# A first gather of four experts straight from unsplit tokens, and a branch hint, in a two-layer attention and MoE kernel

## The chip, the cores and the metric

One core of a Trainium2 chip. The metric is the device time of one execution in microseconds; the engines are TensorE (PE, with its weight loads as PEld), VectorE (DVE), ScalarE (ACT), GpSimd (POOL) and SyncE (SP), which issues the DMAs.

## The reference

A decoder trunk of two layers on 256 tokens of 1024 fp32 values. Each layer has a mixer (three kinds of attention, gated and summed) and a mixture of 16 experts:

```python
for l in range(DEPTH):
    y = mixer(x, w_in[l], a_w_uk[l], a_w_uv[l], c_sinks[l], w_branch[l], w_o[l], cos, sin)
    x = layer_norm(DN_ALPHA * x + y, ln1_g[l], ln1_b[l])
    y = moe(x, router_w, router_b, moe_w_gate[l], moe_w_up[l], moe_w_down[l])
    x = layer_norm(DN_ALPHA * x + y, ln2_g[l], ln2_b[l])

def moe(x, ...):
    aff = sigmoid(xt @ router_w); sel_score = aff + router_b
    # 4 groups of 4 experts: the group whose best two scores sum highest, and in it the best two experts
    ...
    for e in range(N_EXPERTS):
        he = jax.nn.silu(xt @ w_gate[e]) * (xt @ w_up[e])
        y = y + combine[:, e:e + 1] * (he @ w_down[e])
```

w_gate and w_up are 1024 x 512 for each expert, w_down 512 x 1024; all is fp32.

## The kernel before

Everything that is large lives in one pool of 25 slots of 1 MB (8 KB on each partition). Weights come in loads of 1 MB (half of one expert's matrix) in the order of their use, all issued on SP's queue. A load is issued by pump(), as long as fewer than 25 - target["o"] slots hold weights; target["o"] is the number of slots kept for other tiles. put() gives slots back after a product and pumps again. A load waits on SP until the last reader of its slot is done, and at most eight loads are outstanding.

**Mixer's end (L838 to L874).** The last stage adds the output product to the residual in four pieces (half h, token tile t), takes statistics of each (stat), and forms the router's products (logits). ln_scales gives mean and 1/std of a token tile (DVE, then POOL).

**MoE's start (L938 to L1035).** WARM[0] transposes keep PE busy. normed() normalizes a token tile in place (xv is the view [token, tile, q, k], column = 8 q + k), high() casts it to x1h (fp32r, ordered by k), low() forms x1l = x - x1h on POOL and DVE. In between stand the router's steps on DVE: sigmoid (aff), sel, pr, gsum, gmax, gr, best, mx, msk. One product (L1012, `pc`) counts the tokens ahead of each in its expert, and onehot(0) (L1028) turns that into Sx, the one-hots of the first eight experts, 32 places each, for both token tiles.

**gather(r) (L1039).** For eight experts: for each of 8 k and 2 token tiles, a product with x1h[:, t, k] and one with x1l[:, t, k] as the stationary operand (128 x 128, packed) and Sx (256 columns) moving; ACT and DVE evict to xe with LayerNorm's gain and shift. gather(0) runs its first four k ahead of the first gate product and the others behind that product's first half (L1190); gather(1) runs at pair 3 (L1346).

**Main loop (L1311).** For pairs p = 0 to 7 of experts: gate product up_("g", p), up product up_("u", p), each in two halves q of 16 products; tanh and multiplications on ACT and DVE (he); from p = 1 on, down(p - 1), which multiplies by w_down in two halves with turn(p) (transposes of he) between. accumulator(0) at p = 1 has POOL rebuild the tokens as x1h + x1l. slot_maps(0) and turn(0) stand behind the gate product of p = 1. The last down product has rest() between its halves, which issues eight products by an identity (ah, al). At p = 7, over() (L1192) reads a flag and skips, by a branch (tc.If, L1196), a block for experts with more than 32 tokens; in layer 0 this stands behind the last up product, in layer 1 at the start of p = 7. The block is skipped with these inputs.

Each compute instruction goes through a helper, so its line in the profile is L163; each DMA's is L221. A row is told apart by its tile.

Of the kernel before, what the change touches and what calls it, by code (L numbers as in the profile page):

```python
# [18 lines left out]
D = 1024  # L19
# [17 lines left out]
WARM = [38, 6, 12]  # L37
# [167 lines left out]
def kernel(ctx: ExitStack, tc: tile.TileContext, x, w_in, a_w_uk, a_w_uv, c_sinks, w_branch,  # L205
# [28 lines left out]
    def drop(n=1, kind="o"):  # L234
        held[kind] -= n
# [163 lines left out]
    def ln_shift(mean, rstd):  # L399

        sh = small(1, "sh")
        V.scalar_tensor_tensor(sh, mean, -1.0, rstd, op0=OP.mult, op1=OP.mult)
        return sh
# [26 lines left out]
    def mixer(l, todo):  # L430
# [363 lines left out]
        for i, (c, q) in enumerate(stages):  # L794
# [43 lines left out]
            if i == len(stages) - 1:  # L838
                def piece(h, t):

                    cs, ts = slice(256 * h, 256 * h + 256), slice(128 * t, 128 * t + 128)
                    o = pa[c][2 * h + t][:, :256]
                    for kk in range(2):
                        k = 2 * q + kk
                        PE.matmul(o, lh[:, k, ts], hl[:, 0, kk, cs], start=False, stop=False)
                        PE.matmul(o, ll[:, k, ts], hl[:, 0, kk, cs], start=False, stop=False)
                        PE.matmul(o, lh[:, k, ts], hl[:, 1, kk, cs], start=False, stop=(kk == 1))
                    z = xt[0][:, t, 512 + 256 * h:768 + 256 * h]
                    V.scalar_tensor_tensor(z, z, ALPHA, o, op0=OP.mult, op1=OP.add)

                def stat(h, t):
                    V.bn_stats(st[t][:, 12 + 6 * h:18 + 6 * h], xt[0][:, t, 512 + 256 * h:768 + 256 * h])

                halves = (range(2), range(2, 4))
                piece(0, 0)
                piece(0, 1)
                stat(0, 0)
                piece(1, 0)
                stat(0, 1)
                logits(0, 1, 0, halves[0])  # L860
                piece(1, 1)
                logits(1, 1, 0, halves[0])
                logits(0, 1, 0, halves[1])
                stat(1, 0)
                sc = ln_scales(st[:1])
                logits(0, 1, 1, halves[0])
                logits(1, 1, 0, halves[1])
                logits(1, 1, 1, halves[0])
                logits(0, 1, 1, halves[1])
                logits(1, 1, 1, halves[1])  # L870
                stat(1, 1)
                sc += ln_scales(st[1:])
                drop(3)
                return sc, lg, rsum  # L874
# [63 lines left out]
    def moe(l, sc, lg, rsum):  # L938
        target["o"] = 5
        pump()  # L940


        xh = slot([128, T, KD, 128], F32R, "x1h")
        xl = slot([128, T, KD, 128], F32R, "x1l")
        warm(WARM[0])
        xv, hv, lv = xt[0].rearrange("p t (q k) -> p t q k", k=KD), xh.rearrange("p t k q -> p t q k"), \
            xl.rearrange("p t k q -> p t q k")
        halves = [slice(0, 512), slice(512, 1024)]

        def normed(t, k):  # L950
            z = xv[:, t, :, k:k + 4]
            if t == 0:
                V.tensor_scalar(z, z, sc[0][0], sc[0][1], op0=OP.subtract, op1=OP.mult)
            else:
                A.activation(z, z, AF.Identity, bias=sh, scale=sc[1][1])

        def high(t, k):
            A.copy(hv[:, t, :, k:k + 4], xv[:, t, :, k:k + 4])

        def low(E, t, k):  # L960
            E.tensor_tensor(lv[:, t, :, k:k + 4], xv[:, t, :, k:k + 4], hv[:, t, :, k:k + 4].bitcast(F32), op=OP.subtract)

        aff, sel = small(32, "aff"), small(64, "sel")
        z = [aff[:, NE * t:NE * t + NE] for t in range(T)]
        normed(0, 0)
        high(0, 0)
        low(G, 0, 0)
        for t in range(T):
            V.scalar_tensor_tensor(z[t], rsum[:, 0:NE], sc[t][0], lg[t][:, 0:NE], op0=OP.mult, op1=OP.subtract)
        for t in range(T):  # L970
            V.scalar_tensor_tensor(z[t], z[t], sc[t][1], rsum[:, NE:2 * NE], op0=OP.mult, op1=OP.subtract)
        A.activation(aff, aff, AF.Exp)
        sh = ln_shift(*sc[1])
        normed(1, 0)
        normed(0, 4)
        high(0, 4)
        high(1, 0)
        normed(1, 4)
        high(1, 4)
        low(G, 0, 4)  # L980
# [33 lines left out]
        low(V, 1, 0)  # L1014
# [6 lines left out]
        def onehot(r):  # L1021

            Sx[r] = work((128, 8, T, CAP), F32R, name="Sx")
            for t in range(T):
                z = (pos if r else pc)[:, NE * t + 8 * r:NE * t + 8 * r + 8, None].to_broadcast([128, 8, CAP])
                V.tensor_tensor(Sx[r][:, :, t], cc("iota")[:, None, :].to_broadcast([128, 8, CAP]), z, op=OP.is_equal)
# [10 lines left out]
        xe = {}  # L1037

        def gather(r, ks=range(KD)):  # L1039

            if r not in xe:
                z = [slot([128, 4, 8, T, CAP], F32, "xe") for i in range(2)]
                xe[r] = [z[k // 4][:, k % 4] for k in range(KD)]
            for k in ks:
                o = (ptp if k % 2 == 0 else psc)()
                ov_ = o.rearrange("p (e t s) -> p e t s", t=T, e=8)
# [131 lines left out]
        def up_(nm, p, o):  # L1178
            def product(k, a, w):
                x_ = xe[p // 4][k][:, 2 * (p % 4) + a].rearrange("p t s -> p (t s)")  # L1180
                PE.matmul(o[64 * a:64 * a + 64], x_, w, start=(k == 0), stop=(k == KD - 1))

            for q in range(2):
# [5 lines left out]
                if (nm, p, q) == ("g", 0, 0):  # L1189
                    gather(0, range(4, KD))  # L1190

        def over():  # L1192
# [3 lines left out]
            with tc.If(flag > 0):  # L1196
# [8 lines left out]
                with tc.For_i(0, NE, 1) as e:  # L1205
# [5 lines left out]
                    for k in range(KD):  # L1211
                        for j, z in enumerate((xh, xl)):
# [98 lines left out]
        for p in range(NE // 2):  # L1311
            if p == 1:
                target["o"] = 6
            if p == 2:
                target["o"] = 7
# [9 lines left out]
            up_("g", p, pg)  # L1325
            if p == 1:
                slot_maps(0)
                turn(0)
# [14 lines left out]
            if p % 4 == 3:  # L1343
                drop(2)
            if p == 3:
                gather(1)  # L1346
# [60 lines left out]
```

## Time and profile before

| | us |
|---|---|
| median of 3 runs (lowest, highest) | 848.62 (847.47, 849.99) |
| profiled execution | 848.47 |
| its span | 846.70 |
| PE busy | 814.4 (96%) |
| DVE, ACT, POOL busy | 432.5, 289.8, 98.0 |
| DMA moved | 265.27 MB, 313 GB/s over the span |

Times in the rows count from the span's start. Layer 0's experts lie at about 223 to 420 us, layer 1's at about 642 to 847. A busy PE may be one that waits inside: matmuls are pipelined and their ends are modelled.

### The profile page before, as it was taken

The numbers are of one execution on the slowest core, as the hardware profiler recorded it, in microseconds if no ns is written. First come the engines' busy times: TensorE is split into PE (matmuls) and PEld (weight loads), VectorE is DVE, ScalarE is ACT, GpSimd is POOL, SyncE is SP. The second block draws the span as 40 slices with busy tenths as digits, with TensorE's granted clock in tenths as the row PEclk, the third lists the DMA queues.
The fourth block names the chain that finished last, engine by engine and source line by source line (L and its number), as shares of the span: only waits on it lengthen the run. The fifth ranks groups of instructions, "written<-read, shape, count | busy, mean of one in ns | idle before, by whom it ended". The sixth has DMA issues, their size and how long they took to land.

```text
span 846.7 us, 11441 instructions
## 1 busy us (share of the span) xinstructions
PE 814.4 (96%) x4413; PEld 505.8 (60%) x4413; DVE 432.5 (51%) x898; ACT 289.8 (34%) x507; POOL 98.0 (12%) x90
## 2 busy tenths in 40 slices
PE   7999999999999999996989999999999999999896
PEld 7888778888443433332488878788883434333333
DVE  5798665785332323223388977558761412322244
ACT  5545666344111211100355376654341112111112
POOL 1222221002030000000131222110030300000001
PEclk9999999999999999999999999999999999999998
DMA  9993436994799999999896424468947999999992
GB/s 314 345 386 119 138 113 217 379 368 178 266 420 419 420 420 420 420 419 417 319 386 234 158 91 150 150 243 349 357 175 312 420 420 418 419 419 421 416 413 85
DMA packets 65117, 265.27 MB, mean 313 GB/s; under 512 B 6880, under 2 KB 11168, under 8 KB 40992
## 3 DMA queue, kind: packets, MB, share of 16 engines
q1 hardware_dynamic: 64912, 264.39, 80.0%
q8 instruction: 38, 0.62, 0.3%
q14 instruction: 23, 0.19, 0.1%
q10 hardware_dynamic: 144, 0.07, 0.0%
HBM read 263.39 MB, written 1.05 MB: 312 GB/s over the span
## 4 chain that ended last, share of the span: by engine, by line
PE 42%; DMA 7%; DVE 3%; ACT 0%; issue 0%; POOL 0%; POOLq 0%; ACTq 0%; SPq 0%
PE pm L163 36%; DMA w_d<-in_moe_w_down_dram 5%; PE pt L163 3%; PE ps L163 3%; DMA w_u<-in_moe_w_up_dram 2%; DVE bm L163 1%; DVE acc L163 1%; DVE hl L163 0%; POOLq L1403 0%; POOL acc L163 0%; DVE sel L163 0%; ACT hl L163 0%; DVE mv L163 0%; DVE x1l L163 0%; ACT acc L163 0%
## 5 line engine op out<-in xcount | busy, mean ns | idle before, releaser
L163 PE MATMUL pm<-hl,xh 128*128 128x512 f32 (+2 forms) x704 | 226.7, 389 | 1.5 <-ACT hl L163 1.3
L163 PEld LDWEIGHTS pm<-hl,xh 128*128 128x128 f32 x704 | 131.5, 189 | 29.1 <-issue 4.2
L163 DVE TENSOR_TENSOR hl<-w_in,hl 128x1024 fp32r<-128x1024 f32 (+2 forms) x86 | 104.7, 1228 | 60.5 <-ACT hl L163 57.9
L163 PE MATMUL pm<-hl,xl 128*128 128x512 f32 (+2 forms) x352 | 133.9, 380 | 0.3 <-DVE xl L163 0.3
L163 PE MATMUL pm<-w_d,he 128*64 128x512 f32 x512 | 122.2, 609 | 7.1 <-PEq L1196 5.6
L163 PE MATMUL pm<-w_g,xe 128*64 128x512 f32 x512 | 115.0, 594 | 3.6 <-DVEq L1196 1.9
L163 PE MATMUL pm<-w_u,xe 128*64 128x512 f32 x512 | 114.9, 593 | 1.4 <-DMA w_u<-in_moe_w_up_dram 1.4
L163 ACT CAST hl<-w_in 128x1024 fp32r<-128x1024 f32 (+2 forms) x88 | 85.7, 1001 | 5.7 <-DMA w_in<-in_w_in_dram 4.9
L163 PEld LDWEIGHTS pm<-w_d,he 128*64 128x64 f32 x512 | 37.5, 139 | 77.9 <-issue 65.7
L163 PEld LDWEIGHTS pm<-w_g,xe 128*64 128x64 f32 x512 | 37.3, 137 | 76.2 <-issue 72.1
L163 PEld LDWEIGHTS pm<-w_u,xe 128*64 128x64 f32 x512 | 38.7, 137 | 73.2 <-issue 67.6
L163 PEld LDWEIGHTS pm<-hl,xl 128*128 128x128 f32 x352 | 66.9, 190 | 10.1 <-DVE xl L163 0.5
L163 DVE SCALAR_TENSOR_TENSOR he<-he,pm 128x512 f32<-128x512 f32 x16 | 17.0, 1061 | 87.7 <-ACT he L163 79.0
L163 DVE TENSOR_TENSOR he<-he,pm 128x512 f32<-128x512 f32 x16 | 17.1, 1068 | 67.1 <-PE pm L163 67.1
L163 PE MATMUL pm<-hl,mh 128*128 128x256 f32 (+1 forms) x192 | 46.5, 325 | 0.0
L163 ACT COPY he<-pm 128x512 f32<-128x512 f32 x14 | 8.2, 587 | 109.9 <-PE pm L163 109.9
L163 ACT ACTIVATE he<-pm 128x512 f32<-128x512 f32 x16 | 17.3, 1080 | 80.6 <-PE pm L163 80.6
L163 DVE SCALAR_TENSOR_TENSOR yt<-pm,cs,yt 128x512 fp32r<-128x512 f32 x32 | 22.9, 747 | 43.0 <-ACT yt L163 42.1
L163 ACT ACTIVATE yt<-pm,cs 128x512 fp32r<-128x512 f32 x32 | 20.8, 686 | 67.3 <-PE pm L163 67.3
L163 POOL TENSOR_TENSOR un<-un,su 128x512 f32<-128x512 f32 x24 | 30.7, 1285 | 95.2 <-DVE su L163 57.0
L163 PE MATMUL pm<-hl,oh 128*128 128x512 f32 x128 | 41.3, 394 | 0.0
L163 POOL TENSOR_TENSOR rstd<-rs,cst 128x1 f32<-128x1 f32 (+1 forms) x6 | 4.2, 692 | 309.5 <-DVE rs L163 309.5
(198 smaller groups left out, 1034.9 us busy)
## 6 DMA issues: line engine op xcount, KB each, us to landing
w_g<-in_moe_w_gate_dram SPq DMA_DIRECT2D x64, 1024.0 KB, 13.9
w_u<-in_moe_w_up_dram SPq DMA_DIRECT2D x64, 1024.0 KB, 14.6
w_d<-in_moe_w_down_dram SPq DMA_DIRECT2D x60, 1024.0 KB, 19.1
w_in<-in_w_in_dram SPq DMA_DIRECT2D x36, 1024.0 KB, 13.0
w_br<-in_w_branch_dram SPq DMA_DIRECT2D x8, 1024.0 KB, 5.1
w_wo<-in_w_o_dram SPq DMA_DIRECT2D x8, 1024.0 KB, 5.1
w_d<-in_moe_w_down_dram SPq DMA_DIRECT2D x8, 512.0 KB, 17.8
w_in<-in_w_in_dram SPq DMA_DIRECT2D x4, 768.0 KB, 8.1
```

The lines of the kernel that those rows point to most:

```text
L163: r = f(*args, **kw)
```

## The change

The end of the mixer is put in another order: both halves of token tile 0 first, with its statistics, scale and products for the router, then tile 1. At the start of the MoE target["o"] becomes 2 instead of 5, there is no split ahead of the router, and both token tiles are normalized on ACT, 1024 columns at a time. WARM[0] is 32 instead of 38. The first one-hots are made for four experts only. The gather goes in three rounds, of four, four and eight experts. Round 0 takes the tokens unsplit: one fp32 product for each k and token tile, with xv[:, t, :, k], that is every eighth fp32 of a row, as stationary operand and 128 columns moving. Behind the first half of the first gate product come the rest of round 0, the one-hots of the other four experts, and the split to x1h and x1l (apart1, on ACT and DVE). Round 1 runs on PE behind the gate product of p = 1, ahead of turn(0) and slot_maps(0); round 2 where gather(1) was. The tokens' tile stays, so that POOL doesn't rebuild it. target["o"] is 4, 5 (behind the gate product of p = 0), 6 (p = 2), 8 (p = 3) and 16 (p = 7). At p = 6 a branch hint for PE is marked, for the branch of over().

```diff
-WARM = [38, 6, 12]
+WARM = [32, 6, 12]
...
                 piece(0, 0)
+                piece(1, 0)
+                stat(0, 0)
+                logits(0, 1, 0, halves[0])
                 piece(0, 1)
-                stat(0, 0)
-                piece(1, 0)
-                stat(0, 1)
-                logits(0, 1, 0, halves[0])
-                piece(1, 1)
-                logits(1, 1, 0, halves[0])
-                logits(0, 1, 0, halves[1])
                 stat(1, 0)
                 sc = ln_scales(st[:1])
+                logits(0, 1, 0, halves[1])
+                piece(1, 1)
                 logits(0, 1, 1, halves[0])
+                logits(0, 1, 1, halves[1])
+                stat(0, 1)
+                logits(1, 1, 0, halves[0])
+                stat(1, 1)
+                sc += ln_scales(st[1:])
                 logits(1, 1, 0, halves[1])
                 logits(1, 1, 1, halves[0])
-                logits(0, 1, 1, halves[1])
                 logits(1, 1, 1, halves[1])
-                stat(1, 1)
-                sc += ln_scales(st[1:])
...
-        target["o"] = 5
+        target["o"] = 2
...
+        def normed(t):
+            A.activation(xt[0][:, t], xt[0][:, t], AF.Identity, bias=shs[t], scale=sc[t][1])
+
+        shs = [ln_shift(*z, name=f"sh{t}") for t, z in enumerate(sc)]
         for t in range(T):
             V.scalar_tensor_tensor(z[t], rsum[:, 0:NE], sc[t][0], lg[t][:, 0:NE], op0=OP.mult, op1=OP.subtract)
+        normed(0)
         for t in range(T):
             V.scalar_tensor_tensor(z[t], z[t], sc[t][1], rsum[:, NE:2 * NE], op0=OP.mult, op1=OP.subtract)
         A.activation(aff, aff, AF.Exp)
-        sh = ln_shift(*sc[1])
-        normed(1, 0)
-        normed(0, 4)
-        high(0, 4)
-        high(1, 0)
-        normed(1, 4)
-        high(1, 4)
-        low(G, 0, 4)
+        normed(1)
...
-        low(V, 1, 0)
...
-        onehot(0)
+        onehot(0, range(4))
         pos = small(32, "pos")
-        low(G, 1, 4)
         V.tensor_tensor(comb, aff, msk, op=OP.mult)
-        drop()
-        xt[0] = None
         target["o"] = 4
-        pump()
...
+        ROUNDS = [(0, 4), (4, 4), (8, 8)]
...
                 for t in range(T):
-                    PE.matmul(ov_[:, :, t], xh[:, t, k], Sx[r][:, :, t], start=True, stop=False)
-                    PE.matmul(ov_[:, :, t], xl[:, t, k], Sx[r][:, :, t], start=False, stop=True)
+                    m = Sx[e0 // 8][:, e0 % 8:e0 % 8 + n, t]
+                    if r == 0:
+                        PE.matmul(ov_[:, :, t], xv[:, t, :, k], m.bitcast(F32), start=True, stop=True)
+                    else:
+                        PE.matmul(ov_[:, :, t], x1[0][:, t, k], m, start=True, stop=False)
+                        PE.matmul(ov_[:, :, t], x1[1][:, t, k], m, start=False, stop=True)
...
+        def apart1():
+
+            for i, nm in enumerate(("x1h", "x1l")):
+                x1[i] = slot([128, T, KD, 128], F32R, nm)
+            for t in range(T):
+                for k in (0, 4):
+                    h_, l_ = (x1[i][:, t, k:k + 4].rearrange("p k q -> p q k") for i in range(2))
+                    split(h_, l_, xv[:, t, :, k:k + 4])
...
-            if z == 0:
-                xt[0] = slot([128, T, D], F32, "acc")
-                for t in range(T):
-                    h, lo_ = (z[:, t].rearrange("p k q -> p q k").bitcast(F32) for z in (xh, xl))
-                    G.tensor_tensor(xt[0][:, t].rearrange("p (q k) -> p q k", k=KD), h, lo_, op=OP.add)
...
                 if (nm, p, q) == ("g", 0, 0):
                     gather(0, range(4, KD))
+                    onehot(0, range(4, 8))
+                    apart1()
...
-            with tc.If(flag > 0):
+            with tc.If(flag > 0, label=f"over{l}"):
...
         for p in range(NE // 2):
-            if p == 1:
+            if p == 6:
+
+                tc.mark_branch_hint_location(f"over{l}", engines=[mybir.EngineType.PE])
+            if p == 2:
                 target["o"] = 6
-            if p == 2:
-                target["o"] = 7
...
             up_("g", p, pg)
+            if p == 0:
+                target["o"] = 5
             if p == 1:
+                gather(1)
+                turn(0)
                 slot_maps(0)
-                turn(0)
...
             if p == 3:
-                gather(1)
+                gather(2)
```

## Rows read from the trace of the kernel before

**Rows 1.** The page's part 2, the span in 40 equal slices (21.2 us each): busy tenths of PE and mean busy tenths of the 16 DMA engines.

```profile
PE   7999999999999999996989999999999999999896
...
DMA  9993436994799999999896424468947999999992
```

**Rows 2.** The chain of waits in order of time, end of layer 1. Columns: start us, us, what the chain went through.

```profile
763.51 19.89 DMA w_d<-in_moe_w_down_dram
...
803.41 19.91 DMA w_d<-in_moe_w_down_dram
...
823.36 3.65 PE pm L163 x14
...
835.21 2.49 DVE bm L163 x4
```

**Rows 3.** Busy time by stretches. Columns: stretch, its us, busy us of PE, PEld, DVE, ACT and POOL with the number of instructions, the granted clock of TensorE, the DMA share, GB/s.

```profile
610.00:642.00 32.00, 30.11 (x228) 24.69 (x229) 17.05 (x51) 11.92 (x18) 6.87 (x5) 1.00 0.51 182
642.00:830.00 188.00, 183.85 (x938) 71.77 (x936) 55.12 (x82) 28.41 (x38) 7.54 (x2) 1.00 0.99 408
...
625.00:630.00 5.00, 3.41 (x32) 3.17 (x31) 4.67 (x20) 4.31 (x7) 3.80 (x3) 1.00 0.09 39
645.00:650.00 5.00, 5.00 (x26) 1.72 (x24) 0.75 (x1) 0.00 (x0) 0.00 (x0) 1.00 1.01 423
```

**Rows 4.** The timeline of PE and of SP's queue in layer 1 (start us, us, engine, line, operation, out<-in, count), and below it the list of DMA issues for the loads of 642.33 and of 656.11 (the last number is us from issue to landing).

```profile
638.65 3.65 PE L163 MATMUL pm<-w_g,xe 128*64 128x512 f32 x16
...
642.33 0.33 SPq L221 DMA_DIRECT2D w_g<-in_moe_w_gate_dram  x1
...
656.11 0.33 SPq L221 DMA_DIRECT2D w_d<-in_moe_w_down_dram  x1
...
662.40 0.33 SPq L221 DMA_DIRECT2D w_g<-in_moe_w_gate_dram  x1
...
w_g<-in_moe_w_gate_dram SPq DMA_DIRECT2D x1, 1024.0 KB, 5.1
...
w_d<-in_moe_w_down_dram SPq DMA_DIRECT2D x1, 1024.0 KB, 12.5
```

**Rows 5.** The timeline of the router, layer 1 (start us, us, engine, line, operation, out<-in, count, idle time before and what ended it).

```profile
623.41 0.80 POOL L163 TENSOR_TENSOR rstd<-rs,cst 128x1 f32<-128x1 f32 x1 [0.26 <-DVE rs L163]
...
624.81 0.23 ACT L163 ACTIVATE aff<-aff 128x32 f32<-128x32 f32 x1
...
625.09 3.33 POOL L163 TENSOR_TENSOR x1l<-acc,x1h 128x512 fp32r<-128x512 f32 x2 [0.88 <-ACT aff L163]
...
625.67 1.08 DVE L163 TENSOR_TENSOR sel<-aff,rb 128x64 f32<-128x64 f32 x1
...
627.83 0.64 DVE L163 SCALAR_TENSOR_TENSOR best<-gr,sel 128x32 f32<-128x32 f32 x1
...
629.14 0.18 DVE L163 TENSOR_SCALAR msk<-msk 128x32 f32<-128x32 f32 x1
629.23 1.06 DVE L163 TENSOR_TENSOR x1l<-acc,x1h 128x512 fp32r<-128x512 f32 x1
...
629.38 0.41 PE L163 MATMUL pm<-msk,cst 128*128 128x32 f32 x2 [1.59 <-DVE msk L163]
...
630.21 0.75 DVE L163 TENSOR_TENSOR Sx<-cst,pm 128x256 fp32r<-128x256 f32 x2
...
630.77 0.36 PE L163 MATMUL pt<-Sx,x1h 128*128 128x256 f32 x1 [0.29 <-DVE Sx L163]
```

**Rows 6.** Groups of instructions, shapes kept apart, of DVE and ACT. Columns: line, engine, operation, out<-in, shapes, count | busy us, mean ns of one | idle us before.

```profile
L163 DVE TENSOR_TENSOR pr<-sel 128x64 f32<-128x64 f32 x2 | 0.5, 226 | 0.1
...
L163 DVE TENSOR_TENSOR comb<-comb,ssum 128x32 f32<-128x32 f32 x2 | 0.4, 192 | 0.1
...
L163 ACT ACTIVATE he<-pm 128x512 f32<-128x512 f32 x16 | 17.3, 1080 | 80.6 <-PE pm L163 80.6
L163 ACT ACTIVATE th<-pm 128x512 f32<-128x512 f32 x24 | 14.0, 594 | 14.8 <-PE pm L163 13.5
```

**Rows 7.** The timeline of PE, a run of the gather's products, first and last of 12 (layer 1), and small fp32 products in the mixer.

```profile
454.00 0.61 PE L163 MATMUL pt<-uv,wt 128*128 128x128 f32 x4
...
637.12 0.28 PE L163 MATMUL ps<-Sx,x1h 128*128 128x256 f32 x1
...
638.44 0.28 PE L163 MATMUL ps<-Sx,x1l 128*128 128x256 f32 x1
```

**Rows 8.** The branch of L1196 in layer 0: PE's timeline, the stretch of 395 to 400 us (columns as in rows 3), and the DMA queues from 393.2 to 399.2 (queue, kind: packets, MB, share of 16 engines).

```profile
399.40 6.45 PE L163 MATMUL pm<-w_d,he 128*64 128x512 f32 x16 [5.65 <-PEq L1196]
...
395.00:400.00 5.00, 0.60 (x2) 0.33 (x4) 1.26 (x3) 0.00 (x0) 0.00 (x0) 0.83 1.01 416
...
q8 instruction: 1, 0.02, 1.1%
```

**Rows 9.** The end of layer 0: SP's issue of a late load, the DMA issues from 372.2 to 393 (last number: us to landing), and PE's timeline behind the branch.

```profile
384.01 0.33 SPq L221 DMA_DIRECT2D w_d<-in_moe_w_down_dram  x1
...
w_d<-in_moe_w_down_dram SPq DMA_DIRECT2D x5, 1024.0 KB, 19.9
...
413.39 0.50 PE L163 MATMUL ps<-ah,identr 128*128 128x512 f32 x1
...
415.43 3.65 PE L163 MATMUL pm<-w_d,he 128*64 128x512 f32 x16
```

More of the change, by code (lines that the diff above doesn't have):

```diff
@@ L397, in ln_rows, with ln_shift @@
         return p
-    def ln_shift(mean, rstd):
-        sh = small(1, "sh")
+    def ln_shift(mean, rstd, name="sh"):
+        sh = small(1, name)
         V.scalar_tensor_tensor(sh, mean, -1.0, rstd, op0=OP.mult, op1=OP.mult)
@@ L938, in moe @@
     def moe(l, sc, lg, rsum):
-        target["o"] = 5
+        target["o"] = 2
         pump()
-        xh = slot([128, T, KD, 128], F32R, "x1h")
-        xl = slot([128, T, KD, 128], F32R, "x1l")
         warm(WARM[0])
-        xv, hv, lv = xt[0].rearrange("p t (q k) -> p t q k", k=KD), xh.rearrange("p t k q -> p t q k"), \
-            xl.rearrange("p t k q -> p t q k")
+        xv = xt[0].rearrange("p t (q k) -> p t q k", k=KD)
         halves = [slice(0, 512), slice(512, 1024)]
[L950 to L961, printed above, removed]
         aff, sel = small(32, "aff"), small(64, "sel")
         z = [aff[:, NE * t:NE * t + NE] for t in range(T)]
-        normed(0, 0)
-        high(0, 0)
-        low(G, 0, 0)
+        def normed(t):
+            A.activation(xt[0][:, t], xt[0][:, t], AF.Identity, bias=shs[t], scale=sc[t][1])
+        shs = [ln_shift(*z, name=f"sh{t}") for t, z in enumerate(sc)]
         for t in range(T):
             V.scalar_tensor_tensor(z[t], rsum[:, 0:NE], sc[t][0], lg[t][:, 0:NE], op0=OP.mult, op1=OP.subtract)
+        normed(0)
         for t in range(T):
@@ L1019, in moe, with onehot @@
         Sx = {}
-        def onehot(r):
-            Sx[r] = work((128, 8, T, CAP), F32R, name="Sx")
+        def onehot(r, es=range(8)):
+            if r not in Sx:
+                Sx[r] = work((128, 8, T, CAP), F32R, name="Sx")
             for t in range(T):
-                z = (pos if r else pc)[:, NE * t + 8 * r:NE * t + 8 * r + 8, None].to_broadcast([128, 8, CAP])
-                V.tensor_tensor(Sx[r][:, :, t], cc("iota")[:, None, :].to_broadcast([128, 8, CAP]), z, op=OP.is_equal)
-        onehot(0)
+                c = NE * t + 8 * r + es[0]
+                z = (pos if (r, es[0]) != (0, 0) else pc)[:, c:c + len(es), None].to_broadcast([128, len(es), CAP])
+                V.tensor_tensor(Sx[r][:, es[0]:es[-1] + 1, t], cc("iota")[:, None, :].to_broadcast([128, len(es), CAP]), z,
+                                op=OP.is_equal)
@@ L1029, in moe @@
+        onehot(0, range(4))
         pos = small(32, "pos")
-        low(G, 1, 4)
         V.tensor_tensor(comb, aff, msk, op=OP.mult)
-        drop()
-        xt[0] = None
         target["o"] = 4
-        pump()
+        ROUNDS = [(0, 4), (4, 4), (8, 8)]
         xe = {}
+        x1 = {}
         def gather(r, ks=range(KD)):
+            e0, n = ROUNDS[r]
             if r not in xe:
-                z = [slot([128, 4, 8, T, CAP], F32, "xe") for i in range(2)]
-                xe[r] = [z[k // 4][:, k % 4] for k in range(KD)]
+                z = [slot([128, 32 // n, n, T, CAP], F32, "xe") for i in range(n // 4)]
+                xe[r] = [z[k * n // 32][:, k % (32 // n)] for k in range(KD)]
@@ L1044, in gather @@
             for k in ks:
                 o = (ptp if k % 2 == 0 else psc)()
-                ov_ = o.rearrange("p (e t s) -> p e t s", t=T, e=8)
+                ov_ = o[:, :n * T * CAP].rearrange("p (e t s) -> p e t s", t=T, e=n)
                 for t in range(T):
-                    PE.matmul(ov_[:, :, t], xh[:, t, k], Sx[r][:, :, t], start=True, stop=False)
-                    PE.matmul(ov_[:, :, t], xl[:, t, k], Sx[r][:, :, t], start=False, stop=True)
+                    m = Sx[e0 // 8][:, e0 % 8:e0 % 8 + n, t]
[4 more added lines that the diff above has]
+                        PE.matmul(ov_[:, :, t], x1[1][:, t, k], m, start=False, stop=True)
@@ L1179, in product @@
             def product(k, a, w):
-                x_ = xe[p // 4][k][:, 2 * (p % 4) + a].rearrange("p t s -> p (t s)")
+                r = min(p // 2, 2)
+                x_ = xe[r][k][:, 2 * p + a - ROUNDS[r][0]].rearrange("p t s -> p (t s)")
                 PE.matmul(o[64 * a:64 * a + 64], x_, w, start=(k == 0), stop=(k == KD - 1))
@@ L1211, in over @@
                     for k in range(KD):
-                        for j, z in enumerate((xh, xl)):
+                        for j, z in enumerate((x1[0], x1[1])):
                             for t in range(T):
@@ L1342, in moe @@
                 scatter(2, 1)
-            if p % 4 == 3:
-                drop(2)
+            if p in (1, 3, 7):
+                drop(1 + p // 4)
             if p == 3:
-                gather(1)
+                gather(2)
             if p == 7:
```

## The prediction

> **What bounds the kernel now.** First the page's slices by time: TensorE (PE) is busy nearly everywhere, and so is the DMA line in two long stretches, one for each layer's experts [rows 1]. Two full lines don't tell which one sets the pace, so the chain of waits in order of time comes next. From 763.5 us to 823.4 us of layer 1 it holds nothing but loads, one after another, each 19.9 us from issue to landing [rows 2]. SP keeps eight 1 MB loads outstanding, so that is 19.9 / 8 = 2.49 us per MB. The expert stage goes at the pace of the weights, and PE waits between. The tail behind the last load (products, the last LayerNorm on DVE, ACT and POOL) is not touched.
>
> The stretches then say when this bound begins. From 642 to 830 us the DMA share is 0.99, at 408 GB/s; from 610 to 642 it is 0.51, and from 625 to 630, under the router, 0.09 [rows 3]. So the end of layer 1 is a date plus a fixed volume: the date on which the load stream goes full, and then 2.49 us for each MB. That date is SP's issue at 642.33 [rows 4], which takes the slots that the second half of the first gate product (638.65 + 3.65) lets go [rows 4]. Before it there are single loads with pauses, because the slots are full. Every edit here is worth what it does to that date (below: s, per layer), plus any pause that it opens in the stream later. Layer 0 has the same shape [rows 1], and one thing more: behind its last loads PE stands still for 5.65 us at the branch of L1196 [rows 8].
>
> The profiled execution took 848.47 us, 0.15 below the median of 848.62; the sum is made against 848.47.
>
> **Router and first one-hot, which come ahead of that date.** In layer 1 the chain runs: scale of token tile 1 on POOL, exponential, sel, best, msk, a product, the one-hots Sx, first product of the gather at 630.77 [rows 5].
> - POOL's subtractions for x1l (3.33 us for two, beside sel and best) go away. While they run, sel takes 1.08 us and best 0.64; an operation of sel's size outside them takes 0.226, and one of best's size 0.192 [rows 5, 6]. That gives back 0.85 + 0.44 = 1.29.
> - DVE's own x1l of 1.06 us stands between msk and Sx: it ends at 630.29, and the product that Sx needs is done at 629.79. Without it Sx starts 0.35 earlier. Half the columns are enough for four experts: 0.75 for both tiles becomes some 0.5, of which 0.14 ahead of the first product.
> - Against this, both shifts now stand on DVE ahead of the router's four small steps, so these wait for POOL's second scale at 624.21, and ACT does a 1024-wide normalization ahead of the exponential, which was at 624.81. I take 0.45 for both.
> Sum: -1.29 - 0.35 - 0.14 + 0.45 = -1.33; taken -1.3. If DVE is slow for another reason than POOL, only -0.3 is left; if the scale on POOL gets shorter too, -2.0.
>
> The mixer's reordering leaves the number of products ahead of the router the same and moves tile 0's statistics forward; what the router waits for is the last logits and tile 1's scale. Taken 0, bounds -0.5 (tile 0's part no longer late) to +0.5 (tile 1's later). Warming with 32 instead of 38: nothing, PE stands idle for 1.59 us ahead of the product on msk anyway [rows 5]; without this cover a product could start slowed, as behind the branch below.
>
> **The first gather.** Before, eight experts take 32 products per half, two halves; they follow each other at (638.44 - 637.12) / 11 = 0.120 us [rows 7], so a half is 16 x 0.12 and both are 3.84 us. After, four experts take 32 fp32 products of 128 columns in all. Products of this size with a packed stationary operand follow each other at (0.61 - 0.28) / 3 = 0.11, with 0.28 for the last one's own length as in the rows beside it [rows 7]: 32 x 0.11 = 3.5, or -0.3. But the new stationary operand is xv[:, t, :, k], one fp32 of every eight, read by the weight load in steps of 32 bytes. No strided weight load of PE is in this trace. The nearest rows are of ACT and DVE: 512 elements take ACT 1.080 us with a strided side and 0.594 without [rows 6], a factor of 1.8. If the load pays this factor, the pace is 0.11 x 1.82 = 0.20, the gather 6.4 us, and the edit costs +2.6. So its bounds are -0.3 and +2.6. Both halves lie ahead of the date, on PE, where nothing else runs; so the price is paid in full in each layer. I take +2.6, since the rows with a stride all show a price, though on another engine.
>
> The Trainium skill speaks against this edit: SBUF — State Buffer, in the section Door 1: The DMA port swizzle, notes lines of 16 bytes of which at least two accesses should fall into one, each step to a new line being paid. With 32-byte steps every element is on a new line. The strided rows of ACT agree in direction; no row here shows it for PE. By the rule the edit costs about what I take, without it -0.3.
>
> **Second gather, ahead of the second up product.** gather(1) adds 32 products for experts 4 to 7, 32 x 0.11 to 0.12 = 3.5 to 3.8 us of PE per layer, behind the gate product of pair 1. PE has slack in this stage: at 763 to 823 us it waits for loads. But until then the extra time holds back releases. The up product of pair 1 frees its first slots at 662.40 now [rows 4], 20.1 us behind the date; after, it is some 3.5 later, 23.6 behind. The load ahead of it, issued at 656.11, lands 12.5 later, 26.3 behind the date; in a full stream the next is due 2.5 after that, at 28.8. A load that meets an empty queue lands 5.1 after its issue [rows 4], so this one at 23.6 + 5.1 = 28.7: the stream just stays full, and each tenth that the gather or its wait for the split takes longer is a pause. Bounds 0 and 1.1 (a gather 1.2 longer than this); taken +0.5.
>
> **Split moved behind.** Four casts on ACT and four subtractions on DVE, of 1.1 us each as the x1l of [rows 5] (ACT's taken the same), run under the second half of the gate product and the up product of pair 0; they end ahead of gather(1), 7 us later. The tanh of pair 0 may be late by some tenths; who waits for it is the turn in pair 1. If they were late, PE would stand at gather(1), which has a slack as above. Taken 0. POOL's rebuilding of the accumulator is off every chain that ends here; its removal is worth 0.
>
> **Three loads earlier.** Target 5 becomes 2, so three loads go out in the mixer's last part instead of one by one up to 637. SP is ahead of nothing else there. They fill the pauses before the date, but the slots they take are held until the same product frees them: at the date one starts with the same slots to fill. Taken 0, bounds -1 to +1. The later targets only hold back slots for the new tiles.
>
> **Branch hint.** At the branch of L1196, PE's idle time ends by its own sequencer after 5.65 us (393.75 to 399.40), and in the 6 us around it exactly one packet of the instruction queue moves [rows 8]. In the stretch from 395 to 400 the granted clock is 0.83, between its two levels of 1.2 and 2.4 GHz, and the next product of 16 takes 6.45 us instead of 3.65 [rows 4, 8]. The Trainium skill, Runtime: NRT & Kernel Launch, section Instruction fetch mechanics, says that a taken branch to a page outside the window has to fetch it first; the packet agrees. If the hint fetches the page in time, PE goes on at 393.8 at full clock and then waits for loads: the one issued at 384.01 lands 19.9 later, at 403.9 [rows 9]. From there 3.65 for this half of d7, 2.04 for the transposes that stand between (413.39 to 415.43), 3.65 for the last half: 413.25, against 415.43 + 3.65 = 419.08. That is -5.8. Layer 1 starts from there and its mixer is bound by PE, so the gain is carried to the end. If the hint does nothing: 0. In layer 1 the branch lies under a wait for a load, so 0 there.
>
> **The sum.** s = -1.3 + 2.6 + 0.5 = +1.8 per layer. Two layers and the branch: 848.47 + 3.6 - 5.8 = 846.3 us.
>
> **Rivals.**
> - The hint works and the strided load costs nothing: s = -1.3 - 0.3 + 0.5 = -1.1; 848.47 - 2.2 - 5.8 = 840.5. For it: the strided rows are of other engines only, and weight loads overlap with products.
> - Slower: the strided loads cost as above and the branch stays as long as it is: 848.47 + 3.6 = 852.1. It decides from a pace where s passes 0, 32 x pace = 3.84 + 0.8, or 0.145 us per product. For it: the hint stands at pair 6, 20 loads or some 50 us ahead of the branch, and what it fetched may be gone by then.
> - Neither: the hint does nothing and the stride is free: 848.47 - 2.2 = 846.3, the same number by another way. The clock and the gather tell them apart.
>
> **How the numbers follow.** I give the hint 0.75 (one packet and one stall fit what it is for) and the priced stride 0.6. Both: 0.45, my forecast, 846.3. Hint without price: 0.30, 840.5. Price without hint: 0.15, 852.1. Neither: 0.10, 846.3. Each has an uncertainty of some 2 us from the bounds above (router 1 per layer, mixer 0.5, pause 0.5). The range goes from 838.5 (840.5 less 2) to 850.5 (forecast's upper side: two layers by 1.8, with 0.6 for the pause); out of it lie most of the slower rival and the tails, together under 0.2. A measurement can tell 0.3% from no change, 2.5 us here. The forecast lies at -2.2, so its 0.45 splits into 0.21 faster, 0.23 same, 0.01 slower; the second rival counts 0.29 faster and 0.01 same; the slower one 0.10 slower and 0.05 same; neither splits in halves. Together faster 0.55, same 0.34, slower 0.11.
>
> **What would show it.** In the branch's window PE's idle time below 1 us and the clock at 1.00: the hint. The first gather's 32 products: 6.4 us or 3.5. The date of the first issue of the full stream, against the start of the gather: s. A pause in DMA between the up product of pair 1 and its predecessors: the 0.5. What would make me wrong: three early loads that do move the date, or a router whose slow DVE steps stay slow without POOL.

## The result and the profile after

The changed kernel took 854.76 us (median of 12 executions, 850.48 to 856.35), the kernel before 848.95 us; the ratio is 1.0054, 95% interval 1.004 to 1.0069. By the medians it is slower by 5.8 us (the ratio, here and below, is not the quotient of the medians). The forecast was 846.3, and the result lies outside the range. The nearest rival was the slower one, at 852.1.

Its times fall into two groups: five executions from 850.48 to 852.73, seven from 854.72 to 856.35. The profiled execution, 851.32 us, is one of the lower group; what the upper group loses has to be read from another run (below). In all the runs one execution, 1658.2 us, took about twice as long as the seven others of its kernel (842.5 to 847.6, the hint with the moved branch); it is left out, and as it was the profiled one, that kernel has no trace to read.

The last load of the chain now hands over to PE 2.2 us later than in [rows 2] (825.55 for 823.36). The chain of waits, end of layer 1:

```profile
805.58 19.92 DMA w_d<-in_moe_w_down_dram
825.55 3.65 PE pm L163 x14
```

The load stream still sets the end: its share from the date on is 1.00. Busy time by stretches, columns as in [rows 3]; the last is the pause that comes behind the first release of pair 1's up product:

```profile
610.00:643.00 33.00, 32.11 (x213) 26.49 (x213) 14.23 (x53) 11.22 (x17) 1.10 (x2) 1.00 0.45 169
643.00:830.00 187.00, 183.49 (x960) 72.91 (x957) 58.78 (x88) 30.73 (x43) 0.00 (x0) 1.00 1.00 410
667.00:672.00 5.00, 5.00 (x26) 1.72 (x24) 1.70 (x3) 0.00 (x0) 0.00 (x0) 1.00 0.87 321
```

The router is faster, and nearly as was said. Its timeline, to be laid beside [rows 5]:

```profile
622.02 0.55 POOL L163 TENSOR_TENSOR rstd<-rs,cst 128x1 f32<-128x1 f32 x1 [0.93 <-DVE sh L163]
...
624.62 0.23 DVE L163 TENSOR_TENSOR sel<-aff,rb 128x64 f32<-128x64 f32 x1
...
625.92 0.19 DVE L163 SCALAR_TENSOR_TENSOR best<-gr,sel 128x32 f32<-128x32 f32 x1
...
626.79 0.18 DVE L163 TENSOR_SCALAR msk<-msk 128x32 f32<-128x32 f32 x1
```

sel took 1.08 beside POOL and takes 0.23 without it, best 0.64 and 0.19. From tile 1's scale on POOL to the first product of the gather it was 630.77 - 623.41 = 7.36 us and is 627.96 - 622.02 = 5.94: -1.42, forecast -1.3. (That all these times are earlier comes in part from layer 0, which ended 1.2 us sooner in this execution.)

Then the gather gives it back, and more. PE's timeline of its second half, with the date's issue on SP, and the first release of pair 1's up product:

```profile
635.47 1.22 PE L163 MATMUL pt<-Sx,xt 128*128 128x128 f32 x4
636.52 1.12 PE L163 MATMUL ps<-Sx,xt 128*128 128x128 f32 x4
637.48 1.12 PE L163 MATMUL pt<-Sx,xt 128*128 128x128 f32 x4
638.44 1.12 PE L163 MATMUL ps<-Sx,xt 128*128 128x128 f32 x4
639.49 3.65 PE L163 MATMUL pm<-w_g,xe 128*64 128x512 f32 x16
...
643.17 0.33 SPq L221 DMA_DIRECT2D w_g<-in_moe_w_gate_dram  x1
...
666.82 0.33 SPq L221 DMA_DIRECT2D w_g<-in_moe_w_gate_dram  x1
```

Four products start 0.96 us apart ((638.44 - 636.52) / 2), so one takes 0.24 us, twice the 0.12 of [rows 7], although it moves half the columns. From the first product to the date it was 642.33 - 630.77 = 11.56 us and is 643.17 - 627.96 = 15.21: +3.65. So s without the pause is -1.42 + 3.65 = +2.2 per layer. The release comes 666.82 - 643.17 = 23.65 us behind the date (23.6 forecast), and the pause is there: 5 x (1 - 0.87) = 0.65 us by the DMA share, and 5 x (1 - 321 / 410) = 1.1 us by the bytes moved, beside the 410 GB/s of the whole stretch.

### The profile page after: what moved, and what is told of

Its sections match the earlier page's. It is cut to its first block, busy times and chain, and to the rows that moved or that the text cites. A ratio compares the mean times of both kernels' runs of the same rounds, so it can differ in the third digit from the quotient of the medians.

```text
span 848.8 us, 11550 instructions
## 1 busy us (share of the span) xinstructions
PE 823.0 (97%) x4465; PEld 516.8 (61%) x4465; DVE 435.2 (51%) x914; ACT 294.6 (35%) x515; POOL 71.3 (8%) x80
## 5 line engine op out<-in xcount | busy, mean ns | idle before, releaser
L163 PE MATMUL pm<-w_d,he 128*64 128x512 f32 x512 | 119.0, 604 | 4.1 <-DVEq L1187 2.8
L163 ACT ACTIVATE xe<-pt,gpk 128x256 f32<-128x256 f32 (+1 forms) x24 | 15.2, 635 | 65.9 <-PE pt L163 52.5
```

The source lines that it names most:

```text
L163: r = f(*args, **kw)
```

## Experiments

Each time is a median of 6 to 12 executions, the ratio is to the kernel before in the same sitting. "Branch" is PE's branch instruction for the skipped block, of which each layer has one; groups are the two levels of executions described above.

**The hint alone, on the kernel before.**

```diff
-            with tc.If(flag > 0):
+            with tc.If(flag > 0, label=f"over{l}"):
...
+            if p == 6:
+                tc.mark_branch_hint_location(f"over{l}", engines=[mybir.EngineType.PE])
```

> The kernel before with the branch hint alone. Theory: the hint shortens PE's stop at the branch in layer 0 from 5.65 us to about 2.8 us, where DVE's own arrival ends it, and it does so in some executions only; so times in two groups, one at the kernel before (849) and one 3 to 5 us below it (844 to 846). Rival one: the hint works in each execution, one group at 844 to 846. Rival two: it does nothing, one group at 849.

843.69 us, ratio 0.9933 (0.9914 to 0.9952), all within 843.0 to 845.3: rival one. The branch instruction itself, in the kernel before and in this one (min, median and max of the two, ns):

```profile
L1196 PEldq COMPARE_BRANCH  x2: 481/3199/5917, 393.2 to 789.2; - x2
```

```profile
L1196 PEldq COMPARE_BRANCH  x2: 388/524/659, 392.6 to 785.8; - x2
...
L1405 PEldq BRANCH_PREFETCH_HINT  x2: 36/43/50, 0.8 to 393.5; - x2
```

5.92 us became 0.39. What is left of the stop in layer 0, and the stretch around it (columns as in [rows 3]):

```profile
395.98 5.35 PE L163 MATMUL pm<-w_d,he 128*64 128x512 f32 x16 [2.76 <-DVEq L1196]
...
395.00:400.00 5.00, 4.02 (x14) 1.62 (x16) 0.73 (x2) 0.00 (x0) 0.00 (x0) 0.73 1.01 413
```

PE now waits for DVE's arrival instead, 2.76 us, and behind that wait the clock still falls (0.73): the product takes 5.35 us, not the 3.65 of the forecast. So the gain is 4.8 us and not 5.8. The hint doesn't run at pair 6, where it is written: it runs at 0.8 us, at the kernel's start, and for layer 1 at 393.5, just behind layer 0's branch. It holds for 390 us. An instruction packet of queue q8 moves here too, at 396.3, 3.7 us behind the branch, and the branch doesn't wait for it: the one packet of [rows 8] was no sign of a stop by itself.

**The changed kernel without the hint.**

```diff
-            if p == 6:
-                tc.mark_branch_hint_location(f"over{l}", engines=[mybir.EngineType.PE])
```

> The changed kernel without the branch hint. Theory: the two groups of the changed kernel (851 and 855) come from the hint, so one group remains, at 855 to 856, with PE stopped at the branch for 5 to 6 us again. Rival: the two groups come from another place, and both stay.

854.87 us, ratio 1.0052 (1.0024 to 1.008): as the changed kernel, with both groups (850.5 and 851.5; the others 854.7 to 856.1). The theory fell: there are two groups without the hint too, and in the changed kernel's time the hint is worth nothing that can be measured. That the two upper groups are alike isn't shown. This run's profile is of the upper one (854.66); its branches, and below them those of the changed kernel's profile (851.32, lower group):

```profile
L1187 PEldq COMPARE_BRANCH  x2: 1787/3938/6090, 397.2 to 794.9; - x2
```

```profile
L1187 PEldq COMPARE_BRANCH  x2: 348/1068/1787, 395.9 to 792.5; - x2
```

In layer 0 both take 1.79 us. The long branch of this execution, 6.09 us, is that of layer 1, where the changed kernel has 0.35; from layer 1's date to its last product by w_d this execution takes 0.9 us more (192.56 for 191.65). The rest of the 3.3 us between the two executions is a first gather that starts 1.3 us later in layer 0 and a lower clock behind PE's wait there (0.50 for 0.66 from 400 to 405 us).

**A packed stationary operand, by reading other columns.**

```diff
-                        PE.matmul(ov_[:, :, t], xv[:, t, :, k], m.bitcast(F32), start=True, stop=True)
+                        PE.matmul(ov_[:, :, t], xt[0][:, t, 128 * k:128 * k + 128], m.bitcast(F32), start=True, stop=True)
```

> The changed kernel, whose first gather takes 128 columns side by side (columns 128 k to 128 k + 127) in place of every eighth as the stationary operand; so the gathered values are of other columns, the instructions and their waits are the same. Theory: the strided weight load costs the 0.24 us per product; packed, the pace is 0.11 to 0.12, the 32 products take 3.5 to 3.8 us in place of 7.7, and the time falls by 2 x 3.9 = 7.8 us, to 843 to 848. Rival: fp32 products of 128 columns have this pace anyhow, no change.

845.86 us, ratio 0.9961 (0.9943 to 0.9978): 8.9 us less than the changed kernel by the medians, 8.0 by the lower groups (841.6 to 843.3 for 850.5 to 852.7). Instructions of one tile (ns min/median/max), of the changed kernel and of this run:

```profile
L163 PEld LDWEIGHTS pt<-Sx,xt x32: 313/336/338, 209.2 to 638.1; 128*128 128x128 f32 x32
...
L163 PEld LDWEIGHTS pt<-Sx,x1h x32: 186/189/192, 238.1 to 718.4; 128*128 128x128 f32 x32
```

```profile
L163 PEld LDWEIGHTS pt<-Sx,xt x32: 186/192/192, 209.1 to 630.6; 128*128 128x128 f32 x32
```

Other columns are gathered, but the instructions, types and sizes are the same: the stride alone makes a weight load of 128 columns 0.336 us instead of 0.192, and the products, which wait for it, 0.24 apart instead of 0.11. From the first product to the date it is 635.07 - 623.92 = 11.15 us here, 4.06 less than the 15.21 above.

**The second gather behind the up product.**

```diff
             if p == 1:
-                gather(1)
                 turn(0)
...
             if p in (1, 3, 7):
                 drop(1 + p // 4)
+            if p == 1:
+                gather(1)
```

> The changed kernel with the second gather moved behind the up product of pair 1. Theory: its 3.5 us between gate and up product hold back the release that feeds the load stream, a pause of 0.9 us per layer; moved, the pause is gone, and the time falls by 1 to 2 us. Rival: the gather is then late for the gate product of pair 2, PE waits there and holds back other releases, no change or slower.

852.75 us, ratio 1.0042 (1.0024 to 1.006), 2.0 less than the changed kernel. Its profile has the long branch in layer 0 (6.13 us), and it has one group (851.8 to 854.3); set against the changed kernel's upper group alone (median 855.39) it is 2.6 less. The DMA share stays at 1.01 through this part, where it fell to 0.87:

```profile
660.00:665.00 5.00, 5.00 (x36) 3.20 (x34) 2.13 (x6) 2.03 (x3) 0.00 (x0) 1.00 1.01 419
665.00:670.00 5.00, 5.00 (x26) 1.58 (x22) 1.94 (x4) 0.00 (x0) 0.00 (x0) 1.00 1.01 415
670.00:675.00 5.00, 5.00 (x40) 4.06 (x38) 3.70 (x7) 2.26 (x4) 0.00 (x0) 1.00 1.01 421
```

**Eight experts by fp32 from a packed copy.** ACT writes the normalized tokens to a tile xk ordered by k; there is no split.

```diff
-                        PE.matmul(ov_[:, :, t], x1[0][:, t, k], m, start=True, stop=False)
-                        PE.matmul(ov_[:, :, t], x1[1][:, t, k], m, start=False, stop=True)
+                    PE.matmul(ov_[:, :, t], xk[:, t, k], m.bitcast(F32), start=True, stop=True)
```

> The changed kernel with another first gather: ACT writes the normalized tokens once as fp32 into a tile ordered by k, and both gathers take eight experts by fp32 products from this packed tile; no split at all, no gather between gate and up product of pair 1; the hint stays. Theory: the router's gain of about 1.4 us per layer stays, the strided load and the pause go, and PE's instructions stand nearly as in the kernel with the hint alone, so the hint works: 843.7 - 2.8 = 841, one group, 840 to 842. Rival: ACT's strided writes (1.1 us for 512 elements) hold up the exponential and eat the router's gain: 843.5 to 845.

847.94 us, ratio 0.9985 (0.9967 to 1.0003), one group. Neither theory: the exponential is not late, but an fp32 product of 256 columns takes twice one of 128. PE's timeline of the gather in layer 0:

```profile
211.14 1.03 PE L163 MATMUL ps<-Sx,xk 128*128 128x256 f32 x4
212.00 1.03 PE L163 MATMUL pt<-Sx,xk 128*128 128x256 f32 x4
```

(212.00 - 211.14) / 4 = 0.215 each, 6.9 us for the 32, where two-part fp32r products took 3.84 and four experts by fp32 take 3.5.

**Padding of 128 instructions ahead of layer 0's branch.**

```diff
+            if p == 5 and l == 0:
+                z = ptp()
+                for i in range(64):
+                    PE.transpose(z[:32, :128], ident[:, :32], ident)
```

> The changed kernel with 64 small transposes more on PE at the start of pair 5 of layer 0, 128 instructions with their weight loads, some 3.6 us of PE in a stage that waits for loads. Theory: in the changed kernel the branch of layer 0 stands just behind the fetch of a page of instructions, and the hint can't help there; moved by half a page it stands as in the kernel with the hint alone, the branch takes under 0.5 us, and all executions fall into the lower group, 850 to 852. Rival: the two groups have another cause, and stay at 851 and 855, or higher by up to 3.6 us for the padding.

856.09 us, ratio 1.0082 (1.0052 to 1.0112): one group, 855.4 to 858.0, and in its profile layer 0's branch takes 0.39 us. So the place matters, as the theory has it; the time forecast (850 to 852) was wrong, since 64 small transposes take 7.2 us and not 3.6, more than the stage could hide: the branch comes 3.8 us later (399.7 for 395.9).

**The mixer's order of before, and target 5.** Two parts of the change undone, each by itself, in the changed kernel; the first takes back the whole hunk on the mixer's end:

```diff
                 piece(0, 0)
-                piece(1, 0)
-                stat(0, 0)
-                logits(0, 1, 0, halves[0])
                 piece(0, 1)
+                stat(0, 0)
+                piece(1, 0)
...
```

```diff
-        target["o"] = 2
+        target["o"] = 5
```

> The changed kernel with the end of the mixer in the order of the kernel before. Theory: the order is worth nothing (what the router waits for is the last logits and tile 1's scale), within 0.5 us per layer of the changed kernel in each group. Rival: part of the router's 1.5 us comes from the order, and the time rises by 1 to 2 us.

853.48 us, ratio 1.0039 (1.0013 to 1.0065), in both groups about 1 us lower than the changed kernel (the best five 848.96 to 851.56, the others 853.2 to 856.4). The new order costs some 0.5 us per layer, if anything; it is not what made the router faster.

> The changed kernel with target 5 in place of 2 at the start of the MoE, so that the three loads go out later. Theory: no change, since the load stream goes full only when the first gate product's second half frees slots. Rival: the earlier loads take part of the price away, and without them the time rises by 1 to 2 us.

854.79 us, ratio 1.0044 (1.002 to 1.0068): no change. This run's profile caught an execution of the upper group (856.07). PE's timeline behind layer 0's branch, here and in the changed kernel's profile:

```profile
403.48 6.61 PE L163 MATMUL pm<-w_d,he 128*64 128x512 f32 x16 [5.84 <-PEq L1187]
```

```profile
399.29 5.35 PE L163 MATMUL pm<-w_d,he 128*64 128x512 f32 x16 [2.76 <-DVEq L1187]
```

In the upper group the branch takes 6.04 us and PE stands for 5.84, with the hint in place; in the lower one the branch takes 1.79 and DVE ends the wait. Instruction packets: in the lower one the packet comes at 395.2, ahead of the branch at 395.9; in the upper one it comes at 400.6, 3.5 us behind the branch at 397.0.

The fourteen traces agree on how the branch and the packets go together. Either PE's branch takes 0.35 to 0.39 us, or it ends 1.35 to 1.55 us behind the end of a 16 KB instruction packet of queue q8 (that of [rows 8]): it takes 5.9 to 6.3 us where that packet starts 3.4 to 3.8 us behind the branch, 1.8 to 1.9 where it starts 0.6 to 0.8 ahead, 0.5 to 0.7 where it starts 1.9 to 2.0 ahead. Behind the shortest branches a packet comes 3.5 to 3.9 us later all the same, and they don't wait for it.

**The branch moved ahead of the last scatter, in layer 0.**

```diff
             if p == 7:
+                if l < depth - 1:
+                    over()
+                    drop(3)
+                    clk.on = True
                 scatter(2, 1)
```

> The changed kernel with the branch of layer 0 moved ahead of the scatter that follows the last up product; it so stands 32 PE instructions earlier, and DVE has not the scatter's four additions ahead of it. Theory: the branch is then off the fetch of the page behind which it stands now, the hint works (branch under 0.5 us), and DVE's arrival no longer holds PE for 2.8 us; one group at 848 to 850.5. Rival: the two groups don't come from this branch, both stay.

851.14 us, ratio 1.0024 (1.0014 to 1.0035): twelve executions from 850.6 to 851.8. One group, the lower one.

```profile
L1187 PEldq COMPARE_BRANCH  x2: 350/367/384, 392.6 to 792.9; - x2
```

So in the changed kernel the two groups go with this branch: 6.04 and 1.79 us in the two profiles, one group where it is short. The run without the hint, whose upper execution had it at 1.79, isn't covered by this. The time of 848 to 850.5 that the theory gave was not reached: PE's wait for DVE fell from 2.76 to 1.31 us, but the clock, 1.00 behind it (0.66 in the changed kernel, 400 to 405 us), falls to 0.82 and 0.84 at the start of layer 1's mixer instead (425 to 435 us, 1.00 in the changed kernel). Beside the hint alone (843.7), what is left of the change costs 7.4 us, or 3.7 per layer.

> The kernel before with the hint and the branch of layer 0 moved ahead of the scatter. Theory: DVE's arrival is what still holds PE 2.8 us at the branch; with its four additions behind the branch the stop falls below 1.5 us, 842 to 843 in place of 843.7. Rival: behind the branch PE waits for loads soon after, so the time stays at 843.7.

The same move on the kernel with the hint alone: 843.5 us, ratio 0.9949 (0.9929 to 0.9968): nothing gained over 843.7, as the rival had it for the time; whether for its reason, no trace shows.

**Four experts from a packed copy, second gather late, without and with the moved branch.** ACT writes xk as above; the split reads it, and the tokens are normalized in place behind.

```diff
-        target["o"] = 2
+        target["o"] = 3
...
+        xk = slot([128, T, KD, 128], F32, "xk")
...
-                        PE.matmul(ov_[:, :, t], xv[:, t, :, k], m.bitcast(F32), start=True, stop=True)
+                        PE.matmul(ov_[:, :, t], xk[:, t, k], m.bitcast(F32), start=True, stop=True)
```

> The changed kernel with a packed fp32 copy of the normalized tokens for the first four experts (ACT writes it in place of the first normalization, split and in-place normalization follow behind), and the second gather behind the up product of pair 1. Theory: per layer the router's -1.4 and the gather's -0.3 are left, +0 for the pause, so -3.4 against the kernel before; the branch stands where it is in the changed kernel, so the hint helps in some executions or none: 845 without, 841 with it. Rival: the additional slot and ACT work hold up the load stream: above 846 in each execution.

849.15 us, ratio 0.9999 (0.9985 to 1.0013); layer 0's branch takes 6.25 us in the profile. Each execution is above 846 (846.16 to 850.54), as the rival said.

> The same with the branch of layer 0 moved ahead of the scatter as well. Theory: both gains add up, one group at 839 to 841.5, below the kernel with the hint alone (843.7). Rival: with the branch out of the way the load stream is the bound at once, and the moved branch gives nothing over the lower group of the run without it.

845.01 us, ratio 0.9955 (0.9939 to 0.997): the moved branch is worth 4.1 us here, but both came out some 4 us above the sum. Last, the copy without a slot of its own: the tokens' tile is given up once ACT has read it, and the accumulator is filled from xk.

```diff
         packed(1, 4)
+        drop()
+        xt[0] = None
+        target["o"] = 2
+        pump()
...
+            if z == 0:
+                xt[0] = slot([128, T, D], F32, "acc")
```

> As the packed version with late gather and moved branch, but the packed copy costs no slot: the tokens' own tile is given up as soon as ACT has read it, so that the third load goes out early again, and the accumulator is filled from the packed copy by DVE. Theory: the packed version fell short by the one load (2.49 us per MB and layer) that its additional slot keeps back at the date on which the load stream goes full; with the slot back the time is 845.0 - 2 x 2.0 to 2.5 = 840 to 841. Rival: it fell short because the bound has moved to PE, whose second gather and later split still take its time; then it stays at 844.5 to 845.5.

839.02 us, ratio 0.988 (0.9854 to 0.9906): the fastest of all, below both kernels. Ahead of layer 0's date (stretches; first the run with the extra slot, then this one):

```profile
195.00:220.00 25.00, 24.11 (x182) 19.04 (x182) 12.77 (x53) 11.03 (x18) 1.12 (x2) 1.00 0.40 155
220.00:400.00 180.00, 176.96 (x932) 70.85 (x928) 53.79 (x84) 28.62 (x40) 0.00 (x0) 1.00 1.00 414
```

```profile
195.00:220.00 25.00, 24.10 (x181) 18.77 (x181) 13.07 (x53) 10.51 (x17) 1.12 (x2) 1.00 0.50 193
220.00:400.00 180.00, 178.01 (x940) 70.81 (x938) 56.20 (x85) 29.38 (x41) 0.00 (x0) 1.00 1.00 414
```

The date is the same (220.7 and 220.6 us), but 25 x (0.50 - 0.40) = 2.5 us of DMA, one load of 1 MB, now lies ahead of it: SP has issued 23 loads of the experts' weights before the date instead of 22. Two layers give 5, and 6.0 were measured. In the two profiles the stretch from the date to the last product by w_d is shorter by 2.1 us in layer 0 and 2.4 in layer 1; another 1.7 us lies in layer 1's mixer, where the clock of the run with the extra slot fell to 0.66 (425 to 430 us) and this one's stayed at 1.00. The run also leaves out ACT's two normalizations in place; what they cost by themselves no run shows.

## Why the prediction failed

Point by point, by its own steps:

- *The bound* was right: the date plus the volume. The experiments moved the time by what they did to the date, to the pause, to the loads ahead of the date, or to layer 0's branch; beside these the traces show 1 to 2 us by layer 1's branch and by where the clock falls.
- *Router*: -1.3 forecast, -1.42 measured; POOL's part was seen rightly. The term against it, 0.45 without a working, came out at 0.34: the exponential starts 1.74 us behind the start of tile 1's scale instead of 1.40, with the scale itself 0.25 shorter.
- *Mixer's order*: taken 0 within 0.5; the run without it suggests a cost of about 0.5 per layer, at its bound.
- *The first gather*: right mechanism, too small a size. (The prediction's "32 products per half" is a slip: a half is 16, and its sum goes by 16.) The factor of 1.82 on ACT was taken for PE; on PE the pace went from 0.11 to 0.24, a factor of 2.2, and the date moved by 3.65 us from the gather's start instead of 2.6. The bound I set there, +2.6, was no upper bound, and the miss is about 1 us per layer. The Trainium skill (SBUF — State Buffer, Door 1: The DMA port swizzle) spoke against this edit, and the trace agrees in direction: with 32-byte steps each weight load takes 0.336 us for 0.192. It gives no number for PE's loads; the run does.
- *The pause at pair 1*: 0.5 forecast; 0.65 to 1.1 read from the stretch, and 1.0 to 1.3 by the run that moves the second gather (2.0 to 2.6 for two layers).
- *Split moved behind, three loads earlier*: 0 forecast. For the loads the run with target 5 shows 0: by layer 0's date 23 loads are out in both kernels. For the split no run shows it by itself. But I gave as reason that the slots decide, and then didn't price a slot: one slot more or less ahead of the date is 2.1 to 3 us per layer, which the last two runs show.
- *The branch hint, -5.8*: **this is the step that failed.** On the kernel before it was nearly right: -4.8, with PE's wait for DVE's arrival (2.76 us) as what came late next, and with a clock that still fell behind it (0.73), where the step had PE go on at full clock. In the changed kernel its median gains nothing: 854.76 with the hint and 854.87 without. The other parts of the change move the branch within PE's instructions (the trace has 4465 products on PE in place of 4413), and at this place seven executions of twelve lie in the upper group, of which the one profile at hand (of the run with target 5) has a branch of 6.04 us. I treated the parts as a sum; this part depends on where the others put it. Layer 1's branch is 0.35 us in the changed kernel's profile and 6.09 in the one without the hint, so the hint may still serve there; one profile of each doesn't show it. (PE's wait at that branch in the kernel before, 1.89 us, is ended by DVE and not by a load, as the step had it.) That the stop follows the place is shown twice, by padding and by moving the branch. The Trainium skill (Runtime: NRT & Kernel Launch, Instruction fetch mechanics) says that a taken branch out of the window waits for a page. The packets agree: every branch above 0.4 us ends 1.35 to 1.55 us behind the end of a packet, which starts 3.5 us behind the branch in an execution of the upper group and 0.7 us ahead of it in one of the lower. Why the hint doesn't cover this place was not settled: which page holds the target is not in the trace.

So the rival "slower" held in kind: price without hint. With the measured terms it is 848.95 + 2 x (2.2 + 0.65 to 1.3 + 0.5) = 855.7 to 857.0 for an execution with the long branch in layer 0, and 4 to 5 less where it is short; measured are 854.7 to 856.4 and 850.5 to 852.7. I had put 0.15 on it, because one stall and one packet in one trace seemed to vouch for the hint wherever the branch stands. The packet vouched for nothing by itself: it moves behind a short branch too. Of the 8.5 us between forecast and result the hint accounts for 5.8; the rest, 2.7, is mostly the gather (about 1 per layer) and the pause.

## What to carry to other kernels

A strided operand is paid where it is read most: let ACT write the packed order once (four writes of 1.2 to 1.3 us beside the router) instead of letting PE's weight loads step through it 32 times. In a kernel bound by its loads, price every edit by three things: the date on which the stream goes full, the loads out before it (one slot is one load), and releases held back behind it. A branch hint is no fixed gain: measure it in the final instruction order, over several executions, and look at the branch instruction of each layer and not only at the engine's idle time. Before a level of times is put down to one cause, look at a profile of that level: the upper times with and without the hint had their long branch in different layers.

## What the hardware showed that I had not expected

- A weight load of 128 fp32 columns with a 32-byte step takes 0.336 us against 0.192 packed, and its products follow at 0.24 us against 0.11.
- The hint's instruction runs at the start of the program, 0.8 us, and still holds at the branch at 392.6.
- The changed kernel takes 4 to 5 us more or less from execution to execution, and this goes with one branch, whose 16 KB packet of instructions starts 0.7 us ahead of it or 3.5 us behind. A branch that waits ends 1.35 to 1.55 us behind the end of its packet in each of the fourteen traces.
- A shorter stop isn't all gain: with PE's wait cut from 2.76 to 1.31 us the clock stayed at 1.00 there, and fell to 0.82 and 0.84 some 30 us later instead, behind a wait of 1.56 us.
- fp32 products of 256 columns take 0.215 us each, of 128 columns 0.11; fp32r products of 256 take 0.12.
